# A bias table picked by two split products, and gate columns from two transposes of 36 rows

## The chip, the cores and the metric

The kernel runs on one core of one Trainium2 chip. The metric is the device time of one execution in microseconds (us). TensorE (PE) multiplies, VectorE (DVE) and ScalarE (ACT) work elementwise, GpSimd (POOL) does small elementwise work and issues some of the DMAs, and SyncE (SP) issues the loads of the weights. Each engine works through its own instructions in the order in which they are written, and semaphores tie the engines together.

## The reference, cut to what matters

One layer of a hybrid decoder trunk on 256 tokens of width 1024, in float32. Two places matter here. The first is the relative-position bias of the attention branch, a table of 32 buckets and 8 heads, read by the distance of query and key:

```
bias_own = moveaxis(rel_bias[t5_bucket(q_pos[:, None] - k_pos[None, :])], -1, 0)
logit_own = (q_c @ k_own.T) * scale + bias_own          # causal, then softmax
```

The second are the gates of the mLSTM branch: 4 heads with one input and one forget value per token. With F the running sum of log_sigmoid(f) and G = i - F, the kernel takes M as the running maximum of G (from 0), and uses exp(G - M) as weights between tokens and exp(-F - M) as the floor of the denominator:

```
log_f = log_sigmoid(f_pre);  b_cum = cumsum(log_f);  m_q = max(b + m, max(b_l - b_s + i_s))
h = num / max(|den|, exp(-m_q))
```

## The kernel before, in words

All 256 tokens stay on the chip; the weights come as 78 chunks of 1 MB in a fixed order (four chunks "o", then four groups of qm, qb, km, kb, vm, vb, ga, gb, then the branch projections, the output projection and the MLP). A step s of the main loop (L318 to L354) belongs to one chunk: first `elem_work(s)` writes the elementwise work of the chunk before, then chunk s + 2 is split on ACT and DVE into a high and a low float32r part (`wh`, `wl`, written by `split_into`, L91 and L92), then a load is issued, then PE's products of chunk s are written, each as three float32r products (L125 to L127), and last `side_pe[s]`, small PE work at the end of the step. The weights stand in three raw buffers (`raw`), and a buffer is loaded again when its split is done.

What one writes first, an engine does first: the scheduling is manual, and the order on each engine is that of the program. `side_elem[s]` is side work of slot s, behind the elementwise work; `mixed[s]` places side work between the two halves of a split (each `None` is a place for one half).

Around the change the slots are these. Step 3 is the last chunk "o" (result `ps_o`, `ps_o3b`). At its end PE picks the bias table (`ps_rel`, L523): the one-hot array `onehot` (32 x 384, bucket by distance) against `rel` (32 x 8), both float32, both loaded by POOL's DMAs at L227. In slot 4 DVE scales it into `ev` (L528) and POOL issues three DMAs, each of which needs the one before to have landed: `ev` to a table in DRAM (L530), the table spread to a band (`copy_band`, L381), and the band read back as the skewed bias `toe` (`load_band`, L386).

The gates follow beside it: the gate columns of step 3 are transposed at the end of step 4 (`ps_gt`), slot 5 holds `e1`, slot 6 holds `e1b`, a half of the split of chunk 8 (`wl` of chunk vm of group 0), `e1c` (L573 writes G, L574 scans M), the other half, and `e1d` (L578, L579 write -M and nFM = -F - M). All these rows are slices of one tile `gates` on partitions 0 to 3. At the end of step 7 (kb), `p1` transposes G and nFM into columns (`ps_gc`, L586), and step 8 (vm, `ps_vm`) follows on PE. Slots 8 and 9 hold the rest of kb and the first use of the columns (`gcol`, `floor`).

Of the kernel before, what the change touches and what calls it, by code (L numbers as in the profile page):

```python
# [13 lines left out]
AF = mybir.ActivationFunctionType  # L14
# [4 lines left out]
P = 128  # L19
# [6 lines left out]
NB = 32  # L26
# [5 lines left out]
LTOE = 384  # L32
# [37 lines left out]
class Kernel:  # L70
# [446 lines left out]
    def rel_bias_expand(self, rel, onehot):  # L517
        nc = self.nc
        st = {}

        def pe():
            ps = self.ps_side([8, LTOE], "ps_rel")
            nc.tensor.matmul(ps, rel, onehot, start=True, stop=True)  # L523
            st["ps"] = ps

        def elem():
            ev = self.xp.tile([8, LTOE], F32, name="ev")
            nc.vector.tensor_scalar(ev, st["ps"], 1.0 / ATT_SCALE, None, op0=ALU.mult)  # L528
            nc.vector.memset(ev[:, 256:LTOE], NEG)
            nc.gpsimd.dma_start(self.table, ev)  # L530
            self.copy_band(0)
            self.load_band(0)
        self.side_pe.setdefault(3, []).append(pe)
        self.side_elem.setdefault(4, []).append(elem)


    def gates_schedule(self, bif):
        nc, mp = self.nc, self.xp
        st = {}
        v = nc.vector  # L540

        def e0():
            gt = mp.tile([P, 2, 8], F32, name="gt")
            for t in range(2):
                v.tensor_add(gt[:, t, :], self.psg[t][:, 256:264], bif)
            st["gt"] = gt

        def p0():
            ps = self.ps_side([4, 2, S], "ps_gt")
            for w in range(2):  # L550
                for t in range(2):
                    nc.tensor.transpose(ps[:, w, t * P:(t + 1) * P], st["gt"][:, t, 4 * w:4 * w + 4], self.ident)
            st["ps"] = ps

        def e1():
            ps = st["ps"]
            big = mp.tile([P, KT, S], F32, tag="xraw", name="gates")
            fs, t1, F, G, M, nFM, nM = (big[0:4, k, :] for k in range(7))
            v.tensor_copy(fs, ps[:, 1, :])
            v.scalar_tensor_tensor(t1, fs, -1.0, fs, op0=ALU.mult, op1=ALU.min)  # L560
            nc.scalar.activation(t1, t1, AF.Exp)
            nc.scalar.activation(t1, t1, AF.Ln, bias=1.0)
            st["g"] = fs, t1, F, G, M, nFM, nM

        def e1b():
            fs, t1, F, G, M, nFM, nM = st["g"]
            one = self.ones4[:, 0:S]
            v.scalar_tensor_tensor(fs, fs, 0.0, t1, op0=ALU.min, op1=ALU.subtract)
            v.tensor_tensor_scan(F, one, fs, 0.0, op0=ALU.mult, op1=ALU.add)

        def e1c():
            fs, t1, F, G, M, nFM, nM = st["g"]
            v.tensor_sub(G, st["ps"][:, 0, :], F)  # L573
            v.tensor_tensor_scan(M, self.ones4[:, S:2 * S], G, 0.0, op0=ALU.max, op1=ALU.max)  # L574

        def e1d():
            fs, t1, F, G, M, nFM, nM = st["g"]
            v.tensor_scalar(self.nM[0:4, :], M, -1.0, None, op0=ALU.mult)  # L578
            v.scalar_tensor_tensor(nFM, F, -1.0, M, op0=ALU.mult, op1=ALU.subtract)  # L579
            st.update(G=G, nFM=nFM)  # L580

        def p1():
            ps = self.ps_side([P, 2, 2, 4], "ps_gc")
            for w, n in enumerate(("G", "nFM")):
                for t in range(2):
                    nc.tensor.transpose(ps[:, w, t, :], st[n][:, t * P:(t + 1) * P], self.ident[0:4, 0:4])  # L586
            st["gc"] = ps

        def e2():
            self.gcol = self.const.tile([P, 2, 4], F32, name="gcol")  # L590
            self.floor = self.const.tile([P, 2, 4], F32, name="floor")
            v.tensor_copy(self.gcol, st["gc"][:, 0])
            self.floor_exp = lambda: nc.scalar.activation(self.floor, st["gc"][:, 1], AF.Exp)

        b = self.start_g[0]
        self.side_elem.setdefault(b, []).append(e0)
        self.side_pe.setdefault(b, []).append(p0)
        self.mixed[b + 1] = lambda w: w + [None, None, e1]
        self.mixed[b + 2] = lambda w: w + [e1b, None, e1c, None, e1d]
        self.side_pe.setdefault(b + 3, []).append(p1)  # L600
        self.mixed[b + 4] = lambda w: w + [e2]

# [587 lines left out]
```

## Time and profile before

| | |
|---|---|
| median of 3 runs | 490.73 us (490.67 to 490.86) |
| the profiled execution's own time | 490.16 us |
| its span in the profile | 488.4 us |
| PE busy | 477.0 us (98%), 4070 matmuls |
| DVE busy | 369.3 us (76%) |
| ACT busy | 286.2 us (59%) |
| POOL busy | 30.6 us (6%) |
| share of the chain that ended last | PE 97% |

All times of the profile count from the start of the span. A row of the timeline has the start, the time it took, the engine, the line of the program, the operation, what it writes and reads, and how often; in brackets stands how long the engine had been idle before it and what ended the wait. Rows of a queue ("SPq") are issues of DMAs. Matmuls overlap: a product of 256 columns is shown with 0.28 us, but the next one starts 0.12 us later, so the cost of a matmul is the distance between starts.

### The profile page before, as it was taken

To read this page: it belongs to the slowest core of one execution; us is meant where nothing else is said; L and a number is where in the kernel's file an instruction comes from. 1 tells how busy PE (TensorE), PEld (TensorE's weight loads), DVE (VectorE), ACT (ScalarE), POOL (GpSimd) and SP (SyncE) were. 2 spreads that over 40 slices of the span, in tenths; PEclk is the share of its full clock that TensorE was granted. 3 is DMA by queue.
4 is the path that set the end of the run, shared out by engine and by line. 5 is a ranking of instruction groups with operands and counts; after the bars stand their busy time and mean duration, and the time that the engine had idled before them with its cause. 6 is when DMAs were issued, how large, how long until landed. Compare 5 with 4: busy or idle time off the path is not lost.

```text
span 488.4 us, 9811 instructions
## 1 busy us (share of the span) xinstructions
PE 477.0 (98%) x4070; PEld 470.0 (96%) x4070; DVE 369.3 (76%) x659; ACT 286.2 (59%) x476; POOL 30.6 (6%) x46
## 2 busy tenths in 40 slices
PE   8999999999999999999999999999999999999992
PEld 4999999999999999999999999999999999999992
DVE  4967995788588858886677788988668766876886
ACT  5857767495658666856655622767456545654620
POOL 0600011001100110001000001000000000000001
PEclk9999999999999999999999999999999999999997
DMA  8984565555555645543964491827465556454202
GB/s 281 376 299 122 210 196 205 178 180 188 181 191 174 189 160 197 201 150 116 368 231 172 174 344 42 302 89 258 173 236 165 205 173 224 176 204 173 87 2 86
DMA packets 17886, 93.77 MB, mean 192 GB/s; under 512 B 4497, under 2 KB 4889, under 8 KB 7857
## 3 DMA queue, kind: packets, MB, share of 16 engines
q1 hardware_dynamic: 13682, 87.08, 50.1%
q0 software_dynamic: 4160, 6.07, 4.1%
q8 instruction: 32, 0.52, 0.4%
q14 instruction: 12, 0.10, 0.1%
HBM read 92.05 MB, written 2.63 MB: 194 GB/s over the span
## 4 chain that ended last, share of the span: by engine, by line
PE 97%; DMA 1%; DVE 1%; SPq 0%; ACT 0%; issue 0%; POOL 0%; POOLq 0%
PE ps_up L127 8%; PE ps_up L125 8%; PE ps_up L126 8%; PE ffn L127 4%; PE ffn L126 4%; PE ffn L125 4%; PE ps_vm L125 2%; PE ps_qm L125 2%; PE ps_vm L126 2%; PE ps_vm L127 2%; PE ps_ga L125 2%; PE ps_ga L127 2%; PE ps_vb L125 2%; PE ps_vb L126 2%; PE ps_vb L127 2%; PE ps_ga L126 2%
## 5 line engine op out<-in xcount | busy, mean ns | idle before, releaser
L92 DVE TENSOR_TENSOR wl<-raw,wh 128x1024 fp32r<-128x1024 f32 (+1 forms) x162 | 187.7, 1199 | 25.3 <-ACT wh L91 25.2
L91 ACT CAST wh<-raw 128x1024 fp32r<-128x1024 f32 (+1 forms) x162 | 158.4, 1030 | 8.6 <-DMA raw<-in_wst_dram 5.9
L127 PE MATMUL ps_up<-x1h,wl 128*128 128x256 f32 x320 | 88.5, 277 | 0.0
L126 PE MATMUL ps_up<-x1l,wh 128*128 128x256 f32 x320 | 88.5, 276 | 0.0
L125 PE MATMUL ps_up<-x1h,wh 128*128 128x256 f32 x319 | 88.3, 277 | 0.0
L126 PEld LDWEIGHTS ps_up<-x1l,wh 128*128 128x128 f32 x320 | 60.2, 188 | 0.0
L127 PEld LDWEIGHTS ps_up<-x1h,wl 128*128 128x128 f32 x320 | 60.1, 188 | 0.0
L125 PEld LDWEIGHTS ps_up<-x1h,wh 128*128 128x128 f32 x319 | 59.9, 188 | 0.0
L1020 DVE SCALAR_TENSOR_TENSOR cu<-ps_up,vec,cu 128x255 f32<-128x255 f32 (+1 forms) x80 | 33.1, 476 | 23.1 <-ACT cu L1016 23.0
L127 PE MATMUL ffn<-wh,hl 128*128 128x256 f32 (+1 forms) x170 | 47.7, 281 | 0.0
L126 PE MATMUL ffn<-wl,hh 128*128 128x256 f32 (+1 forms) x170 | 47.7, 281 | 0.0
L125 PE MATMUL ffn<-wh,hh 128*128 128x256 f32 (+1 forms) x170 | 47.7, 281 | 0.0
L91 ACT CAST hh<-cu 128x256 fp32r<-128x256 f32 x22 | 8.9, 407 | 42.9 <-DVE cu L1028 42.9
L126 PEld LDWEIGHTS ffn<-wl,hh 128*128 128x128 f32 x170 | 32.0, 188 | 0.3
L125 PEld LDWEIGHTS ffn<-wh,hh 128*128 128x128 f32 x170 | 31.9, 188 | 0.3
L127 PEld LDWEIGHTS ffn<-wh,hl 128*128 128x128 f32 x170 | 31.9, 188 | 0.3
L1016 ACT ACTIVATE cu<-ps_up,vec 128x256 f32<-128x256 f32 x40 | 16.7, 469 | 25.7 <-PE ps_up L127 25.7
L125 PE MATMUL ps_gb<-xth,wh 128*128 128x256 f32 x64 | 18.0, 282 | 0.0
L126 PE MATMUL ps_vm<-wl,xth 128*128 128x256 f32 x64 | 17.9, 280 | 0.0
L127 PE MATMUL ps_vm<-wh,xtl 128*128 128x256 f32 x64 | 17.9, 280 | 0.0
L927 POOL TENSOR_TENSOR rs<-rs,mhalf 128x1 f32<-128x1 f32 x4 | 2.7, 666 | 242.4 <-DVE rs L926 242.4
L125 PE MATMUL mix<-wh,mgh 128*128 128x256 f32 x64 | 17.8, 279 | 0.0
(295 smaller groups left out, 1441.7 us busy)
## 6 DMA issues: line engine op xcount, KB each, us to landing
raw<-in_wst_dram SPq DMA_DIRECT2D x78, 1024.0 KB, 4.9
raw<-in_wst_dram SPq DMA_DIRECT2D x5, 512.0 KB, 8.0
lnrow<-in_rows_dram POOLq DMA_DIRECT2D x4, 512.0 KB, 6.8
band<-table POOLq DMA_DIRECT2D x4, 384.0 KB, 12.2
toe<-band POOLq DMA_DIRECT2D x4, 256.0 KB, 4.4
xtok<-in_x_dram POOLq DMA_DIRECT2D x1, 1024.0 KB, 7.7
out_dram<-r SPq DMA_DIRECT2D x3, 256.0 KB, 2.0
raw<-in_wst_dram SPq DMA_DIRECT2D x2, 256.0 KB, 3.8
```

The costliest lines, as they stand in the source:

```text
L91: self.nc.scalar.copy(wh, raw)
L92: self.nc.vector.tensor_sub(wl, raw, wh.bitcast(F32))
L125: mm(ps, ah if first is None else first, bh, start=start, stop=False)
L126: mm(ps, ah, bl, start=False, stop=False)
L127: mm(ps, al, bh, start=False, stop=stop)
L927: nc.gpsimd.tensor_tensor(st["rs"], st["rs"], self.mhalf[:, 0:1], op=ALU.pow)
L1016: act.activation(cu[:, j, :], ps[:, j, :], AF.Copy, scale=tap(2, j))
L1020: v.scalar_tensor_tensor(cu[:, j, o:], ps[:, j, :S - o], tap(t, j), cu[:, j, o:], op0=ALU.mult, op1=ALU.add)
```

## The change

The bias table is now picked by two float32r products. A new piece `cut`, in slot 3, makes their operands in tiles that are not in use yet: POOL copies `onehot` as float32r into `picks`, a part of `vmh`, and ACT and DVE split `rel` into a high part `rh` and a low part `rl`, two slices of `vml`. At the end of step 3 PE multiplies `rh` by `picks` and adds `rl` by `picks`.

The columns of the gates now come by two transposes. nFM moves from partitions 0 to 3 of its own slice to partitions 32 to 35 of the slice that holds G, so that 36 rows hold both; POOL fills these 36 rows with zeros first (a memset in `e1`), and `p1` transposes 36 rows twice, once for each half of the tokens, in place of 4 rows four times. The reads of the columns change with it.

```diff
@@ rel_bias_expand
+        half = LTOE // 2
+        picks = self.vmh[0:NB, :, 0:half]
+        rh, rl = (self.vml[0:NB, 0, i:i + 8] for i in (0, 8))
+        def cut():
+            nc.gpsimd.tensor_copy(picks, onehot.rearrange("p (a b) -> p a b", a=2))
+            self.split_into(rh, rl, rel)
         def pe():
             ps = self.ps_side([8, LTOE], "ps_rel")
-            nc.tensor.matmul(ps, rel, onehot, start=True, stop=True)
+            nc.tensor.matmul(ps, rh, picks, start=True, stop=False)
+            nc.tensor.matmul(ps, rl, picks, start=False, stop=True)
...
+        self.side_elem.setdefault(3, []).append(cut)
@@ gates_schedule
-            fs, t1, F, G, M, nFM, nM = (big[0:4, k, :] for k in range(7))
+            fs, t1, F, G, M, _, nM = (big[0:4, k, :] for k in range(7))
+            nFM = big[32:36, 3, :]
+            nc.gpsimd.memset(big[0:36, 3, :], 0.0)
+            st["both"] = big[0:36, 3, :]
...
-            ps = self.ps_side([P, 2, 2, 4], "ps_gc")
-            for w, n in enumerate(("G", "nFM")):
-                for t in range(2):
-                    nc.tensor.transpose(ps[:, w, t, :], st[n][:, t * P:(t + 1) * P], self.ident[0:4, 0:4])
+            ps = self.ps_side([P, 2, 36], "ps_gc")
+            for t in range(2):
+                nc.tensor.transpose(ps[:, t, :], st["both"][:, t * P:(t + 1) * P], self.ident[0:36, 0:36])
...
-            v.tensor_copy(self.gcol, st["gc"][:, 0])
-            self.floor_exp = lambda: nc.scalar.activation(self.floor, st["gc"][:, 1], AF.Exp)
+            v.tensor_copy(self.gcol, st["gc"][:, :, 0:4])
+            self.floor_exp = lambda: nc.scalar.activation(self.floor, st["gc"][:, :, 32:36], AF.Exp)
```

Three places of the order follow, each row an instruction with its line, what it writes and reads, and in brackets the semaphores on which it waits (Pool, DVE, PE and Activation are engines, DMASW and DMAHW are DMAs). Lines below the change are 9 to 12 higher in the changed kernel.

POOL's instructions from the end of the set-up to the first DMA of the bias and past it, first before, then changed:

```order
L291 MEMSET mhalf 128x2
L530 DMA table<-ev 8x384 [waits DVE_49]
L381 DMA band_195<-table 256x1x384 [waits DMASW4_49]
L386 DMA toe<-band_195 128x2x256 [waits DMASW5_49]
L633 AFFINE_SELECT wt_781<-wt_781 128x256 [waits DMASW3_49,DMAHW0_49,DMASW2_49,DMAHW3_49,DVE_49,DMAHW4_49,PE_49,DMAHW5_49,Activation_49,Pool_49]
```

```order
L291 MEMSET mhalf 128x2
L527 CAST vmh<-onehot 32x2x192 [waits DMASW3_49]
L540 DMA table<-ev 8x384 [waits DVE_49]
L381 DMA band_195<-table 256x1x384 [waits DMASW4_49]
L386 DMA toe<-band_195 128x2x256 [waits DMASW5_49]
L571 MEMSET gates 36x256 [waits DMAHW5_49,DMAHW0_49,Activation_49]
```

The copy of the one-hot array stands ahead of the three DMAs of the bias, and the memset of the gates' tile stands behind all three.

DVE's instructions of slot 6, from the two parts of qb to nFM and the taps of km, first before, then changed (`wl_539` and `wl_544` are the low part of chunk 8):

```order
L470 SCALAR_TENSOR_TENSOR qbl<-ps_qb_489,vec,qbh 128x128
L568 SCALAR_TENSOR_TENSOR gates<-gates 4x256 [waits DVE_49]
L569 SCALAR_TENSOR_TENSOR gates<-ones_190,gates 4x256 [waits DVE_49,Pool_49]
L92 TENSOR_TENSOR wl_539<-raw_338,wh_538 128x1024 [waits DMAHW2_49,Activation_49]
L573 TENSOR_TENSOR gates<-ps_gt,gates 4x256 [waits DVE_49]
L574 SCALAR_TENSOR_TENSOR gates<-ones_190,gates 4x256 [waits DVE_49,Pool_49]
L92 TENSOR_TENSOR wl_539<-raw_338,wh_538 128x1024 [waits Activation_49]
L578 TENSOR_SCALAR nM<-gates 4x256 [waits DVE_49]
L579 SCALAR_TENSOR_TENSOR gates<-gates 4x256
```

```order
L582 SCALAR_TENSOR_TENSOR gates<-gates 4x256 [waits DVE_49]
L583 SCALAR_TENSOR_TENSOR gates<-ones_190,gates 4x256 [waits DVE_49,Pool_49]
L92 TENSOR_TENSOR wl_544<-raw_341,wh_543 128x1024 [waits DMAHW2_49,Activation_49]
L587 TENSOR_TENSOR gates<-ps_gt,gates 4x256 [waits DVE_49,Pool_49]
L588 SCALAR_TENSOR_TENSOR gates<-ones_190,gates 4x256 [waits DVE_49]
L92 TENSOR_TENSOR wl_544<-raw_341,wh_543 128x1024 [waits Activation_49]
L592 TENSOR_SCALAR nM<-gates 4x256 [waits DVE_49]
L593 SCALAR_TENSOR_TENSOR gates<-gates 4x256
L430 TENSOR_SCALAR cvkm<-cbuf,vec 128x256 [waits Activation_49] x2
```

The instructions stand as before; the one that writes G (L573, now L587) waits for POOL as well as for DVE.

PE's instructions at the two changed places of the changed kernel, the end of step 3 and the end of step 7:

```order
L127 MATMUL ps_o3b<-wh_234,xtl 128x264
L532 MATMUL ps_rel<-vmh,vml 8x384 [waits Activation_49,Pool_49]
L533 MATMUL ps_rel<-vmh,vml 8x384 [waits DVE_49]
L125 MATMUL ps_qm_416<-xth,wh_268 128x256
...
L127 MATMUL ps_kb_636<-xth,wl_471 128x256
L598 MATMUL ps_gc<-ident,gates 128x36 [waits DVE_49,Pool_49]
L598 MATMUL ps_gc<-ident,gates 128x36
L125 MATMUL ps_vm_715<-wh_543,xfirst 128x256 [waits PE_49,Activation_49]
```

Before, one `ps_rel` row that waits for two DMAs stood in the first place, and four `ps_gc` rows in the second.

More of the change, by code (lines that the diff above doesn't have):

```diff
@@ L579, in e1d @@
             v.scalar_tensor_tensor(nFM, F, -1.0, M, op0=ALU.mult, op1=ALU.subtract)
-            st.update(G=G, nFM=nFM)
         def p1():
-            ps = self.ps_side([P, 2, 2, 4], "ps_gc")
-            for w, n in enumerate(("G", "nFM")):
-                for t in range(2):
-                    nc.tensor.transpose(ps[:, w, t, :], st[n][:, t * P:(t + 1) * P], self.ident[0:4, 0:4])
+            ps = self.ps_side([P, 2, 36], "ps_gc")
+            for t in range(2):
+                nc.tensor.transpose(ps[:, t, :], st["both"][:, t * P:(t + 1) * P], self.ident[0:36, 0:36])
             st["gc"] = ps
```

## The prediction

> **What bounds the kernel now.** I read the page first, then who waits for whom on PE, then the timeline of each engine around the two changed places.
>
> ```profile
> PE 477.0 (98%) x4070; PEld 470.0 (96%) x4070; DVE 369.3 (76%) x659; ACT 286.2 (59%) x476; POOL 30.6 (6%) x46
> PE 97%; DMA 1%; DVE 1%; SPq 0%; ACT 0%; issue 0%; POOL 0%; POOLq 0%
> PE warm_ps L194 <- DVE warm L191: 1.2, 1, 1.2
> PE ps_o L159 <- ACT wh L91: 1.2, 1, 1.2
> ```
>
> PE carries 97% of the chain that ended last, and the last two rows, all of the waits view for PE, say that it waits twice, both in the first 8 us. So each microsecond that PE gains or stands still between there and its last product is a microsecond of the end, unless a later wait swallows it. POOL, 6% busy, looks harmless, but the change gives it two instructions that others wait for. Its timeline:
>
> ```profile
> 21.03 0.50 POOL L227 DMA_DIRECT2D onehot<-in_onehot_dram  x1
> 21.53 0.30 POOL L249 CAST xfirst<-xth 128x128 fp32r<-128x128 f32 x1
> 21.87 0.32 POOL L284 MEMSET nM<- 128x256 f32 x1
> 34.02 0.53 POOL L530 DMA_DIRECT2D table<-ev  x1 [11.31 <-DVE gt L545]
> 39.62 1.14 POOL L381 DMA_DIRECT2D band<-table  x1 [5.08 <-DMA table<-ev]
> 53.50 0.76 POOL L386 DMA_DIRECT2D toe<-band  x1 [12.73 <-DMA band<-table]
> ```
>
> Not the busy time but the brackets are to be seen: POOL itself stands 5.08 us for the table and 12.73 us for the band, because it holds each issue until the DMA before has landed. What is written behind the issue of toe does not start before 53.50 + 0.76 = 54.26.
>
> **The bias product.** Before:
>
> ```profile
> 27.65 2.36 DVE L92 TENSOR_TENSOR wl<-raw,wh 128x1024 fp32r<-128x1024 f32 x2 [1.97 <-ACT wh L91]
> 28.76 0.29 PE L127 MATMUL ps_o3b<-wh,xtl 128*128 128x264 f32 x1
> 28.99 0.80 PE L523 MATMUL ps_rel<-onehot,rel 32*8 32x384 f32 x2
> 29.72 0.39 PE L125 MATMUL ps_qm<-xth,wh 128*128 128x256 f32 x1
> 29.95 0.28 PE L126 MATMUL ps_qm<-xtl,wh 128*128 128x256 f32 x1
> 30.07 0.28 PE L127 MATMUL ps_qm<-xth,wl 128*128 128x256 f32 x1
> DMA to landing us min/median/max: 7.8/7.8/7.8
> 33.67 0.14 DVE L545 TENSOR_TENSOR gt<-ps_o3b,bif 128x8 f32<-128x8 f32 x1
> ```
>
> From 28.76 to 29.72 is 0.96, less one ordinary step of 0.12: the float32 pick costs 0.84 us. Two float32r products of 384 columns cost 1.5 ordinary steps each, 2 x 0.18 = 0.36, so with ready operands the edit gains about 0.5. They are not ready. `rl` is written by DVE behind the split that ends at 27.65 + 2.36 = 30.01; with 0.14 for a piece of 8 columns (the last row) it is there at 30.15, so PE's second product starts then and ps_qm at 30.35: 0.65 us later than now. `picks` needs onehot, landed at 21.03 + 7.8 = 28.83 (the row before the last); the cast of 128 columns took 0.30, so 384 take at most 0.9 and end at 29.7, ahead of `rl`. Bounds: -0.5 if nothing were late, +1.2 if the cast were twice as slow. I take +0.65. As the next part shows, it does not reach the end: PE runs into a longer wait 22 us later, whose end does not depend on PE.
>
> **The gates' columns.** Before, on DVE and then on PE:
>
> ```profile
> 48.11 0.40 DVE L573 TENSOR_TENSOR gates<-ps_gt,gates 4x256 f32<-4x256 f32 x1
> 48.62 0.68 DVE L574 TENSOR_TENSOR_SCAN gates<-ones,gates 4x256 f32<-4x256 f32 x1
> 49.22 1.19 DVE L92 TENSOR_TENSOR wl<-raw,wh 128x1024 fp32r<-128x1024 f32 x1
> 50.54 0.41 DVE L579 SCALAR_TENSOR_TENSOR gates<-gates 4x256 f32<-4x256 f32 x1
> 51.95 0.28 PE L127 MATMUL ps_kb<-xth,wl 128*128 128x256 f32 x1
> 52.15 0.40 PE L586 MATMUL ps_gc<-ident,gates 4*128 4x4 f32 x4
> 52.49 0.39 PE L125 MATMUL ps_vm<-wh,xfirst 128*128 128x256 f32 x1
> 79.48 0.44 PE psy L705 x4
> ```
>
> Four transposes of 4 rows took 52.49 - 52.15 = 0.34, 0.085 each; the last row, from the chain, has 0.11 for one with 128 columns. Two with 36 lie between: 0.17 to 0.22, a gain of 0.12 to 0.17 on PE. I take 0.15.
>
> The price is the memset. G lies in the slice that it clears, so DVE's write of G waits for POOL, and the memset is written behind the issue of toe. When does it end? The small split on DVE moves ev, and so the table and the band, by 0.14. Against that stands the second of these loads of 1 MB, issued when the second half of the split of chunk 8 ends (49.22 + 1.19), beside the last 3 us of the band:
>
> ```profile
> 41.39 0.33 SPq L86 DMA_DIRECT2D raw<-in_wst_dram  x1
> 50.44 0.33 SPq L86 DMA_DIRECT2D raw<-in_wst_dram  x1
> DMA to landing us min/median/max: 10.4/12.2/14.7
> ```
>
> That split will be late, so the load is not there, and the band may land sooner. The last row is the four bands': 10.4 to 14.7 us. Here the issue of toe came 53.50 - 39.62 = 13.9 behind that of the band; I take 13.5, with the row's ends as bounds. Then toe is issued at 53.50 + 0.14 - 0.4 = 53.25 and done at 54.0, the memset of 256 columns takes 0.32 (the nM row), and G starts at 54.4 in place of 48.11: DVE is 6.3 us late. It stands there, and behind G stand M, the second half of chunk 8, nFM, the taps of km and the next splits. nFM ends at 50.54 + 0.41 + 6.3 = 57.25. PE comes to its transposes at 51.95 + 0.12 + 0.65 = 52.7 and waits 4.55 us; after 0.2 for two transposes vm starts at 57.5, not 52.49: **+5.0 us**. The earliest landing, toe at 39.62 + 0.14 + 10.4 = 50.15, gives +1.9, the latest, 54.45, +6.2.
>
> Does DVE's 6.3 hurt PE again, which is only 5.0 late?
>
> ```profile
> 56.66 0.67 DVE L92 TENSOR_TENSOR kml<-cvkm,kmh 128x512 fp32r<-128x512 f32 x1
> 59.17 0.28 PE L127 MATMUL pss<-qmh,kml 128*128 128x256 f32 x1
> 57.26 0.86 DVE L470 SCALAR_TENSOR_TENSOR kbl<-ps_kb,vec,kbh 128x256 fp32r<-128x256 f32 x2
> 59.98 0.28 PE L126 MATMUL psl<-kbl,qbh 128*128 128x256 f32 x1
> ```
>
> The first uses of km and kb behind vm have 59.17 - 57.33 = 1.84 and 59.98 - 58.12 = 1.86 us of slack; 1.3 of it goes, nothing is left over to wait for.
>
> **The clock.** PE will stand for 4.55 us, and before it never stood that long, except at the very end:
>
> ```profile
> 1.25 3.94 PE L194 MATMUL warm_ps<-warm 128*128 128x512 bf16 x10 [1.25 <-DVE warm L191]
> 8.27 0.23 PE ps_o0b L159
> 6.40:8.00 1.60, 0.41 (x2) 0.23 (x2) 0.68 (x2) 1.21 (x3) 0.00 (x0) 1.00 1.02 380
> 479.00:479.50 0.50, 0.45 (x4) 0.24 (x3) 0.06 (x2) 0.00 (x0) 0.00 (x0) 1.00 0.00 0
> 482.00:482.50 0.50, 0.00 (x0) 0.00 (x0) 0.50 (x3) 0.40 (x1) 0.02 (x1) 0.91 0.00 0
> 482.50:483.00 0.50, 0.00 (x0) 0.00 (x0) 0.50 (x3) 0.00 (x0) 0.50 (x1) 0.50 0.00 0
> ```
>
> In the last rows PE stops at 479.45 and the granted clock is 0.50 from 482.4 on, 3.0 us later; in the gap of 1.4 us at 6.4 to 8.0 it stayed 1.00. At the start ten products of 512 columns took 3.94 us, some 0.4 each, where 0.23 is the rate later (second row): half rate for the first 3.5 us of work. So I expect a fall in the wait and half rate behind it. Bounds: nothing, if the clock holds, and half of 3.5, 1.75. The wait is nearer to the end's gap, so I take 1.5, a little under the upper bound since some of the wait may count. [...]
>
> **The sum.** +5.0 + 1.5 = +6.5. The profiled execution took 490.16 us (span 488.4 and 1.8 around it), which makes 496.7; the median of the runs is 0.57 higher, 490.73, which makes **497.2**.
>
> **The rivals.**
> - The clock holds: +5.0, 495.7. For it: nothing in the trace shows a wait of 4 to 5 us followed by work; against it the end rows. [...]
> - The band lands after 10.4 us, as in its best case: the wait on PE shrinks to 1.5 us, the clock stays, +1.9, 492.6. At the median, 12.2, +3.7 and 494.4, more if the clock falls. For it: half of the four bands landed below 12.2. Against it: the load issued at 41.39 runs beside this band as before.
> - Not slower: POOL passes the memset while the issue of toe waits, so that G is not held. It would need POOL's 12.73 idle microseconds to be spent in the DMA queue and not on the engine. Then only +0.65 - 0.15 = +0.5 is left, 491.2, no change by measure; it decides for any memset that ends before 48.8. Against it stands that POOL's row of toe itself starts only at 53.50.
> - Worse: a second wait behind the first, where DVE or ACT, 6.3 us late, miss a deadline that I have not seen, above 498.6.
>
> **How the numbers follow.** Forecast 60% (its own range 496.2 to 498.6), the clock holds 17%, the band early 12%, not slower 6%, worse 5%. The range 493.6 to 498.6 leaves out the last two and half of the early band, a little under 2 in 10. About 0.2%, 1.0 us, is what a measurement of this kernel can tell from no change. All but the third rival are slower by more: 0.93 with a bit of its own doubt; same 0.05; faster 0.02, since even both gains without any wait, 0.5 + 0.15, stay under 1.0.
>
> **What would show it.** After: POOL's memset behind the issue of toe near 54; DVE idle for 5 to 6 us before it writes G, released by POOL; PE idle for 4 to 5 us before ps_gc, released by DVE; a granted clock of 0.50 in the following microseconds; a wait of about 1.2 us before the second ps_rel product; and no other wait on PE. The prediction is wrong if G starts before 50, or if PE waits again after 60.

## The result, and the profile after

The changed kernel takes 496.71 us in the median of 4 runs (495.66 to 497.68); the kernel before took 490.70 in the runs beside it. The ratio is 1.0119, 95% interval 1.0107 to 1.0131: 6.0 us slower, where +6.5 was forecast. One of the 36 runs of the kernel before beside the experiments took 2760.59 us and is left out of every comparison.

The chain and the waits of PE in the changed kernel (what was waited for, the us in total, how often, the longest). Lines in the gates' part are up to 14 higher than before: the writes of G and nFM, L573 and L579 before, are L587 and L593 here.

```profile
PE 87%; DVE 2%; POOL 0%; issue 0%; POOLq 0%
PE ps_gc L598 <- DVE gates L593: 3.9, 1, 3.9
PE warm_ps L194 <- DVE warm L191: 1.2, 1, 1.2
PE ps_o L159 <- ACT wh L91: 0.9, 1, 0.9
PE ps_rel L533 <- DVE vml L92: 0.5, 1, 0.5
PE ps_rel L532 <- ACT vml L91: 0.2, 1, 0.2
```

Where PE waited twice, it now waits five times, and one wait is larger than all others together: the two transposes of the gates wait 3.9 us for nFM. No later wait of PE stands in the list, so what is lost there is lost at the end. POOL's timeline names the cause, DVE's shows how it is passed on:

```profile
39.66 1.15 POOL L381 DMA_DIRECT2D band<-table  x1 [4.17 <-DMA table<-ev]
53.63 0.76 POOL L386 DMA_DIRECT2D toe<-band  x1 [12.83 <-DMA band<-table]
54.38 0.34 POOL L571 MEMSET gates<- 36x256 f32 x1
```

```profile
54.75 0.41 DVE L587 TENSOR_TENSOR gates<-ps_gt,gates 4x256 f32<-4x256 f32 x1 [4.96 <-POOL gates L571]
57.21 0.42 DVE L593 SCALAR_TENSOR_TENSOR gates<-gates 4x256 f32<-4x256 f32 x1
```

The memset, 0.34 us of work, starts when the issue of toe is through, and DVE stands idle for 4.96 us before G, since what is written behind G on DVE stays behind it. PE's rows, and one row for each stretch of time with the busy time of PE, its weight loads, DVE, ACT and POOL and then the granted clock, show the two parts of the price (the first two rows stand on both sides of the bias pick and are used further down):

```profile
29.76 0.29 PE L127 MATMUL ps_o3b<-wh,xtl 128*128 128x264 f32 x1
31.34 0.39 PE L125 MATMUL ps_qm<-xth,wh 128*128 128x256 f32 x1
53.57 0.28 PE L127 MATMUL ps_kb<-xth,wl 128*128 128x256 f32 x1
57.77 0.40 PE L598 MATMUL ps_gc<-ident,gates 36*128 36x36 f32 x2 [3.93 <-DVE gates L593]
58.10 0.58 PE L125 MATMUL ps_vm<-wh,xfirst 128*128 128x256 f32 x1
60.40 0.41 PE L126 MATMUL ps_vm<-wl,xth 128*128 128x256 f32 x1
60.61 0.41 PE L127 MATMUL ps_vm<-wh,xtl 128*128 128x256 f32 x1
65.00 0.59 PE L625 MATMUL psw<-nM,ident 128*128 128x256 f32 x2
```

```profile
56.00:57.00 1.00, 0.00 (x0) 0.00 (x0) 1.00 (x2) 0.00 (x0) 0.00 (x0) 1.00 0.11 41
57.00:58.00 1.00, 0.23 (x2) 0.26 (x2) 0.95 (x4) 0.00 (x0) 0.00 (x0) 0.79 0.13 16
60.00:61.00 1.00, 1.00 (x6) 1.00 (x6) 1.00 (x3) 0.32 (x1) 0.00 (x0) 0.51 1.00 418
61.00:62.00 1.00, 1.00 (x11) 1.00 (x10) 1.00 (x2) 1.00 (x3) 0.00 (x0) 1.00 0.11 33
```

vm starts at 58.10 where it started at 52.49: +5.6. Then the clock, fallen at about 57.6, stays at one half until 61.0, and products start 0.21 us apart (60.40 to 60.61) in place of 0.12. The next step, psw, starts at 65.00, 6.90 us behind vm's first product. In the kernel before, its row is this one:

```profile
58.06 0.59 PE L613 MATMUL psw<-nM,ident 128*128 128x256 f32 x2
```

That was 58.06 - 52.49 = 5.57 us behind: +1.3. Together +6.9, which is the difference of the two profiled executions' own times, 497.10 and 490.16. The runs differ by 6.0, since the profiled execution before was 0.5 us faster than the median of the runs beside the result and the one of the changed kernel 0.4 slower than its own.

### The profile page after: what moved, and what is told of

It reads as the page before. It is cut to its first block, busy times and chain, and to the rows that moved or that the text cites. A ratio compares the mean times of both kernels' runs of the same rounds, so it can differ in the third digit from the quotient of the medians.

```text
span 495.4 us, 9810 instructions
## 1 busy us (share of the span) xinstructions
PE 479.5 (97%) x4068; PEld 471.7 (95%) x4068; DVE 370.5 (75%) x660; ACT 286.5 (58%) x477; POOL 31.8 (6%) x48
## 4 chain that ended last, share of the span: by engine, by line
PE 87%; DVE 2%; POOL 0%; issue 0%; POOLq 0%
PE ps_up L126 8%; PE ps_up L127 8%; PE ps_up L125 8%; PE ffn L126 4%; PE ffn L127 4%; PE ffn L125 4%; PE ps_vm L125 2%; PE ps_vm L126 2%; PE ps_vm L127 2%; PE ps_ga L125 1%; PE ps_ga L127 1%; PE ps_vb L125 1%; PE ps_vb L126 1%; PE ps_vb L127 1%; PE ps_ga L126 1%; PE mix L125 1%
```

## The experiments

The theory is that of the prediction: the memset stands in POOL's order behind an issue that POOL holds until the band has landed; G, and behind it nFM and PE's transposes, wait for it; the wait lets the clock fall. The rivals are that the layout of 36 rows itself is slow, that the split bias product has a share in the loss, that the clock costs nothing, and that PE waits for something shorter than the whole chain behind G. "Before" is 491.09 us in both sets of runs beside the experiments (490.42 to 492.29), 0.4 above the 490.70 beside the result, and the changed kernel was not run again beside them. So each experiment is set against 491.09, and the changed kernel's +6.0 against 490.70.

**The memset one place up.** Same memset, same engine, between the issue of band and the issue of toe:

```diff
             self.copy_band(0)
+            self.gates = self.xp.tile([P, KT, S], F32, tag="xraw", name="gates")
+            nc.gpsimd.memset(self.gates[0:36, 3, :], 0.0)
             self.load_band(0)
...
-            big = mp.tile([P, KT, S], F32, tag="xraw", name="gates")
+            big = self.gates
-            nc.gpsimd.memset(big[0:36, 3, :], 0.0)
```

> The changed kernel with the same memset on the same engine, written one place further up: between the issue of band and the issue of toe. Theory (the memset stands behind POOL's wait for the band): it ends near 41, DVE writes G with no wait on POOL, PE does not wait before ps_gc, the clock stays at 1.00; what is left is about +0.6 us at ps_rel (1.46 us from the last ps_o3b step to ps_qm, where before had 0.84) and about -0.15 us at ps_gc, so 491.2 us, within 0.2% of before. Rival (the 36-row layout itself is slow: memset of 36 rows, G and nFM in one slice, 36-wide transposes): 495 us or more, as in the changed kernel.

Measured: 491.45 us, ratio to before 1.0007 (0.9998 to 1.0016). Its rows of POOL, DVE, PE and the waits:

```profile
40.57 1.14 POOL L381 DMA_DIRECT2D band<-table  x1 [5.30 <-DMA table<-ev]
41.71 0.34 POOL L543 MEMSET gates<- 36x256 f32 x1
```

```profile
49.51 0.41 DVE L588 TENSOR_TENSOR gates<-ps_gt,gates 4x256 f32<-4x256 f32 x1
```

```profile
53.35 0.28 PE L127 MATMUL ps_kb<-xth,wl 128*128 128x256 f32 x1
53.56 0.31 PE L599 MATMUL ps_gc<-ident,gates 36*128 36x36 f32 x2
53.80 0.39 PE L125 MATMUL ps_vm<-wh,xfirst 128*128 128x256 f32 x1
```

```profile
PE warm_ps L194 <- DVE warm L191: 1.2, 1, 1.2
PE ps_o L159 <- ACT wh L91: 1.0, 1, 1.0
PE ps_rel L533 <- DVE vml L92: 0.4, 1, 0.4
```

The memset ends at 42.05, G's row has no bracket, the wait before ps_gc is gone, and with it 5.6 of the 6 us. psw starts 5.56 us behind vm's first product (59.36 and 53.80), as before. The layout of 36 rows is not slow; the place of the memset in POOL's order was what cost.

**Only the gates.** The kernel before with the second part of the change alone (`rel_bias_expand` as before).

> The kernel before with only the second part of the change (zeroed slice of 36 rows, two transposes), the bias still picked by one float32 product. Theory: the whole loss is here, and the 0.6 us of the bias part is swallowed by the wait before ps_gc, so 496 to 497.5 us, the same as the changed kernel. Rival (the two parts add up, each with its own share of the loss): clearly under 496.7, by 0.6 us or more at equal landing of the band.

Measured: 496.98 us, ratio 1.0137 (1.0106 to 1.0168), with four runs from 495.96 to 499.84. The wait is there with about the same size, and so is the fall of the clock, at 58.0:

```profile
52.48 0.28 PE L127 MATMUL ps_kb<-xth,wl 128*128 128x256 f32 x1
56.83 0.28 PE L587 MATMUL ps_gc<-ident,gates 36*128 36x36 f32 x2 [4.08 <-DVE gates L582]
57.05 0.39 PE L125 MATMUL ps_vm<-wh,xfirst 128*128 128x256 f32 x1
```

```profile
57.00:58.00 1.00, 1.00 (x10) 0.96 (x10) 1.00 (x4) 0.00 (x0) 0.00 (x0) 0.99 0.81 131
58.00:59.00 1.00, 1.00 (x7) 1.00 (x6) 1.00 (x4) 0.00 (x0) 0.00 (x0) 0.50 0.98 410
```

So the second part alone makes a loss as large as the whole. That the bias part adds exactly nothing to it cannot be read from the times, whose interval is 3 us wide.

**Only the bias.** The kernel before with the first part alone (`gates_schedule` as before).

> The kernel before with only the first part of the change (two split products for the bias). Theory: PE waits about 0.5 us for the low part of rel behind the split of chunk 5 on DVE, and nothing swallows it, so ps_qm comes 0.6 us later and the time is 491.3 us (+0.6, 0.12%). Rival 1 (the split products gain as their arithmetic says): 490.2 us. Rival 2 (the pick is late enough to push the band and toe): over 492 us.

Measured: 491.31 us, ratio 1.0004 (0.9996 to 1.0013): no change that can be told, and the expected +0.6 us (1.0012) is still inside the interval. The profile says more than the time. In this execution there is no wait at ps_rel:

```profile
30.31 0.15 DVE L92 TENSOR_TENSOR vml<-rel,vml 32x8 fp32r<-32x8 f32 x1
```

```profile
30.37 0.29 PE L127 MATMUL ps_o3b<-wh,xtl 128*128 128x264 f32 x1
30.59 0.34 PE L532 MATMUL ps_rel<-vmh,vml 32*8 32x384 f32 x1
30.76 0.33 PE L533 MATMUL ps_rel<-vmh,vml 32*8 32x384 f32 x1
31.03 0.38 PE L125 MATMUL ps_qm<-xth,wh 128*128 128x256 f32 x1
```

PE came to ps_rel when the low part of rel was there, since it was 1.6 us later than in the profile before (30.37 against 28.76 for the product ahead of the pick). Only 0.3 us of that are longer waits in the waits view; the rest was not followed up. The pick then costs 31.03 - 30.37 - 0.12 = 0.54 us, 0.3 less than the float32 pick. In the changed kernel's execution it cost 31.34 - 29.76 - 0.12 = 1.46.

**PE kept at work.** The changed kernel, with 14 products of zeros ahead of the transposes; their result is not used:

```diff
+        self.warm = warm
...
         def p1():
+            hold = self.ps_side([P, 512], "ps_hold")
+            for _ in range(14):
+                nc.tensor.matmul(hold, self.warm[:, :P], self.warm, start=True, stop=True)
```

> The changed kernel with 14 extra products of zeros (bfloat16, 512 columns, 0.23 us each, 3.2 us in all) on PE ahead of the two transposes, inside the wait of about 4 us, so that PE works while it would stand. Theory of the clock (the wait lets the clock fall and 1.5 of the 6 us are half rate): granted clock stays 1.00, vm runs at 0.12 us a product from its first, and the time is 1.0 to 1.7 us under the changed kernel: 495.0 to 495.7 us. Rival (the fall costs nothing, all of the loss is the wait): the same as the changed kernel, 496.7 us; if the extra products outlast the wait: more.

Measured: 495.21 us, ratio 1.0094 (1.0073 to 1.0115). Against before that is +4.1 us where the changed kernel has +6.0, but the intervals overlap, and one of the four runs took 497.48, with a mean granted clock of 0.990 against 0.995 or 0.996 in the other three, so that the clock may have fallen there. The profile says more. PE stands idle for 0.76 us only, because it works in most of what was the wait, and the clock holds (the profile shows 13 of the 14 products):

```profile
53.56 2.97 PE L599 MATMUL ps_hold<-warm 128*128 128x512 bf16 x13
57.29 0.28 PE L602 MATMUL ps_gc<-ident,gates 36*128 36x36 f32 x2 [0.76 <-DVE gates L594]
57.50 0.38 PE L125 MATMUL ps_vm<-wh,xfirst 128*128 128x256 f32 x1
63.05 0.59 PE L629 MATMUL psw<-nM,ident 128*128 128x256 f32 x2
```

```profile
58.00:59.00 1.00, 1.00 (x11) 1.00 (x11) 1.00 (x4) 0.00 (x0) 0.00 (x0) 1.00 0.62 262
```

Eleven products run between 58 and 59, where the changed kernel ran six or seven in a microsecond, and psw starts 63.05 - 57.50 = 5.55 us behind vm's first product: 5.57 before, 6.90 in the changed kernel. So the fall of the clock is a part of the loss of its own, 1.3 us behind vm's start and 0.1 at the transposes. Not all of the 1.9 us between the two kernels' times is the clock: psw comes 1.95 us earlier than in the changed kernel, and 0.5 of that is a memset that ended at 54.24 and not at 54.72, because the band landed sooner in this execution.

**The split ahead of G.** The changed kernel, with the second half of chunk 8's split on DVE before G and not behind M:

```diff
-        self.mixed[b + 2] = lambda w: w + [e1b, None, e1c, None, e1d]
+        self.mixed[b + 2] = lambda w: w + [e1b, None, None, e1c, e1d]
```

> The changed kernel with one move on DVE: the second half of the split of chunk 8 (1.19 us) ahead of G instead of behind M, so that DVE does it while it waits for the memset. The memset stays behind the issue of toe. Theory (PE waits for the chain memset, G, M, split, nM, nFM): the chain is 1.1 us shorter, the wait before ps_gc 2.7 instead of 3.9 us, and the time 1.1 us shorter, 495.6 us; where the shorter wait leaves the clock at 1.00 as well, 494.1 us. Rival (PE waits for the memset alone, or for the split of chunk 8): the wait and the time are the same as in the changed kernel.

Measured: 496.13 us, ratio 1.0101 (1.0086 to 1.0116), +5.0 us against before. The chain is shorter by the split, as the theory says, but the clock falls all the same, at 57.4:

```profile
54.04 0.34 POOL L571 MEMSET gates<- 36x256 f32 x1
55.87 0.41 DVE L593 SCALAR_TENSOR_TENSOR gates<-gates 4x256 f32<-4x256 f32 x1
56.43 0.28 PE L598 MATMUL ps_gc<-ident,gates 36*128 36x36 f32 x2 [2.96 <-DVE gates L593]
```

```profile
57.00:58.00 1.00, 1.00 (x9) 1.00 (x8) 1.00 (x3) 0.00 (x0) 0.00 (x0) 0.70 0.00 0
58.00:59.00 1.00, 1.00 (x7) 1.00 (x6) 1.00 (x4) 0.00 (x0) 0.00 (x0) 0.50 0.00 0
```

From the end of the memset to the end of nFM 56.28 - 54.38 = 1.90 us pass, where the changed kernel has 57.63 - 54.72 = 2.91; so the rival, a wait for the memset alone, falls. The wait shrank from 3.9 to 3.0 us and the time by about 1.0, though the intervals of the two times overlap, and 0.3 us of what this profiled execution gained is a band that landed sooner. The price of the clock did not shrink: psw starts 7.19 us behind vm's first product here (63.83 and 56.64), 7.18 with the gates alone (64.23 and 57.05), against 5.57 before, which is 1.6.

**Both edits without their waits.** The kernel with the memset one place up, with the pick moved into the middle of qm, where its operands are ready:

```diff
-        self.side_pe.setdefault(3, []).append(pe)
-        self.side_elem.setdefault(4, []).append(elem)
+        def pick():
+            pe()
+            elem()
+        self.pick = pick
...
-        self.mm_feat(s, ps, self.xth, self.xtl)
+        self.mm_feat(s, ps, self.xth, self.xtl, self.pick if n == "qm" and g == 0 else None)
```

> memset_up with the bias pick moved from the end of step 3 into the middle of step 4 (qm of group 0, behind its first 24 products, 2.8 us later), and the scaling of ev and the three DMAs moved behind it. The memset stands ahead of the issue of toe. Theory (the pick is cheap when the low part of rel is ready): no wait on PE at ps_rel, the two products cost about 0.5 us in place of 0.84, the two transposes about 0.25 in place of 0.34, no other wait on PE: 0.4 to 0.6 us under before, 0.1%, at the edge of what can be told. Rival 1 (0.2 us or more of the bias chain is now on the path, toe lands late for the first logits on DVE): at or over before. Rival 2 (a switch of operand kinds in the middle of a stream of products costs as much as it saves): equal to before.

Measured: 491.04 us, ratio 0.9995 (0.9986 to 1.0004): inconclusive, the gain that was expected and none are both inside. The rows give its size:

```profile
33.06 0.28 PE L127 MATMUL ps_qm<-xth,wl 128*128 128x256 f32 x1
33.27 0.33 PE L532 MATMUL ps_rel<-vmh,vml 32*8 32x384 f32 x1
33.44 0.33 PE L533 MATMUL ps_rel<-vmh,vml 32*8 32x384 f32 x1
33.71 0.39 PE L125 MATMUL ps_qm<-xth,wh 128*128 128x256 f32 x1
53.20 0.28 PE L127 MATMUL ps_kb<-xth,wl 128*128 128x256 f32 x1
53.41 0.31 PE L602 MATMUL ps_gc<-ident,gates 36*128 36x36 f32 x2
53.65 0.39 PE L125 MATMUL ps_vm<-wh,xfirst 128*128 128x256 f32 x1
```

The pick costs 33.71 - 33.06 - 0.12 = 0.53 us in place of 0.84, the transposes 53.65 - 53.20 - 0.12 = 0.33 in place of 0.42. Both edits do what they say, and it is 0.4 us in all. This version does not lose what the changed kernel loses; that it beats the kernel before is not shown.

## Why the prediction was right

- **The bound.** It held. Nothing behind vm catches up what is lost there: PE's last product ends 6.9 us later than before (486.38 against 479.45), as psw started 6.9 us later. Of the +5.6 at vm, PE was 1.6 late already when it reached the end of kb (53.57 against 51.95), 0.6 by the pick and 1.0 by a slower start of this execution. The wait swallowed both: its end is set by POOL, whose issue of the band stands at 39.66, against 39.62 before.
- **The memset behind POOL's held issue**, the step that carried the forecast, is shown by the place alone: one row up in POOL's order, and 5.6 of 6 us are gone. The rival that POOL passes the memset while the issue waits falls with the row at 54.38.
- **The size of the wait.** +5.0 was forecast for vm, +5.6 measured. Mis-sized was the landing of the band: 0.4 us were taken off because the load at 50.44 would be missing. It was missing, yet the issue of toe came 53.63 - 39.66 = 14.0 behind that of the band, not 13.5, and nFM ended at 57.63, not 57.25. The other 0.2 us lie between nFM's end and vm: 0.1 until the first transpose starts, and the transposes, which ran at the fallen clock and took 0.33, not 0.2. The wait itself was 3.9 us, not 4.55, since PE came to it 1.0 later than forecast.
- **The clock.** 1.5 was taken; 1.3 was measured in the changed kernel and 1.6 in the two others in which the clock fell, under the upper bound of 1.75. That the fall comes inside the wait, as forecast, held by 0.2 us in this execution and not in those two, where it came 1 us after PE was back at work; that the size is close all the same is in part luck. Half of the 3.4 us that the half rate lasted is 1.7 at most.
- **The bias product.** +0.65 was forecast up to ps_qm, +0.62 measured in the changed kernel (1.46 less 0.84). That this is so close is luck. The pair of products with ready operands costs 0.53, not 0.36, and the waits are no constant: where about 1 us of waiting follows from the prediction's rows, and 1.2 was named as a sign, the changed kernel has 0.5 for `rl` and 0.2 for `rh`, which had been put at nothing. The wait for `rl` was 0.4 and 0.2 us in two other profiled executions and absent in two more with the pick at the same place, since both PE's arrival there and the end of the split ahead of `rl` differ from execution to execution. That the loss does not reach the end, as the prediction said, fits the run with the gates alone.
- **The transposes.** A gain of 0.15 was taken, 0.09 measured at full clock. In the changed kernel's execution the two took as long as the four before (0.33 from 57.77 to 58.10, against 0.34), because the clock had fallen.
- **The sum.** The mechanism is right in each of its steps; that 497.2 and 496.71 are so close is in part luck. The two profiled executions differ by 6.9, 0.4 more than the forecast, and the medians by 6.0, 0.5 less, because single executions of both kernels scatter by up to 2 us.

The runs of the changed kernel spread over 2.0 us, those of the kernel before beside it over 0.26, but over 1.9 us beside the experiments. The wait's end hangs on the landing of a DMA: in the four profiles with the memset behind toe it ended between 53.79 and 54.72. Whether this, the clock or the start-up makes the spread was not tried.

## What to carry to other kernels

An engine that also issues DMAs is a queue, and POOL's 6% of busy time said nothing about when its next instruction would start: the same memset of 0.34 us ended at 54.72 behind the held issue of toe, at 42.05 ahead of it. Before something small is given to it, read in its timeline what stands ahead, above all an issue that waits for another DMA to land. Where the main engine never waits, a new wait can cost more than its length: here waits of 3.0 to 4.1 us cost 1.3 to 1.6 us on top, because the clock fell too, and shortening the wait by a quarter did not bring that part back. A gain of 0.4 us from cheaper instructions is only worth its operands if these are ready without a new wait.

## What the runs showed of the hardware that was not expected

The half rate lasted 3.4 us each time: from 57.6 to 61.0 in the changed kernel, from 58.0 to 61.4 with the gates alone, from 57.4 to 60.8 with the split ahead of G. In the last two it set in when PE was back at work: with the gates alone PE resumed at 56.83, with the split ahead of G at 56.43, after a wait of 3.0 us. So the end of the wait did not tell when the fall came, and a shorter wait did not mean a shorter half rate.

A pair of small products in a stream of large ones cost more than its own two steps: with the pick in the middle of qm the two products start 0.17 us apart (33.27 and 33.44), but 0.53 us pass in all, so 0.2 are left beside them. The transposes fit this: halving their number brought 0.09 of 0.42 us. Whether 36 rows in place of 4 took a part of that gain was not tried.
